# A two-layer hybrid trunk: 1024 output columns of layer one and the gates of layer two computed with tokens in rows, then turned and regrouped through DRAM

## The chip, the cores and the metric

The kernel runs on 1 core of one Trainium2 chip. The metric is device time in microseconds (us), the median of 3 runs. The profile is of one more execution of the same program, taken by the hardware profiler.

## What is computed

The input is x with 256 tokens of 2048 features, in f32. Two layers follow, each h = h + Mixer(RMSNorm(h)). The reference, cut to what matters here:

```python
# layer one (mixer A): gated DeltaNet with 16 heads of 128
proj = hn @ a_w_in                       # 2048 -> 8224: q, k, v (conv, SiLU), gate z, two scalars a head
o    = delta_rule(q, k, v, decay, beta)  # chunks of 64 tokens
h    = h + (rms_norm(o) * silu(z)) @ a_w_out          # 2048 -> 2048
# layer two (mixer B): chunked attention with 16 heads of 128
proj = rms_norm(h) @ b_w_in              # 2048 -> 8192: q, k, v, gate z
q, k = rms_norm(q), rms_norm(k)
p    = softmax(q @ k.T * scale + bias[relative distance], masked)
h    = h + ((p @ v) * silu(z)) @ b_w_out              # 2048 -> 2048
```

## The kernel before

**Chunks.** All four weight matrices are streamed once from DRAM in 320 chunks of 512 KB. A table, `plan`, lists them in order, and `chunk` consumes one after the other. A weight is split into two fp32r numbers: ScalarE casts it (`whi`, line 207), VectorE takes the difference (`wlo`, line 208), and TensorE adds three products, hi times hi, hi times lo and lo times hi (the matmuls of line 256). There are four buffers for `wt` and three each for `whi` and `wlo`. SyncE's DMA queue carries all weight loads. `fetch` runs three chunks ahead of the matmuls in the program.

**Three forms of a chunk.** Each covers 1024 weights of a partition and streams 6144 columns through TensorE:

- "features" (features in rows, tokens in columns): 24 matmuls of 256 columns, the weights stationary;
- "half" (features in rows): 8 matmuls of 512 columns, in which the high weights meet both parts of the activations at once, and 8 of 256. The two parts of the result are added afterwards by `joined` (ScalarE line 326, VectorE line 327);
- "tokens" (tokens in rows, features in columns): 12 matmuls of 512 columns, the activations stationary.

Counting from 0, the chunks of before are 0 to 7 features, 8 to 63 half, 64 to 87 tokens, 88 to 119 half, 120 to 127 tokens (all `a_w_in`), 128 to 143 features and 144 to 159 half (`a_w_out`), 160 to 191 half (gates of layer two), 192 to 255 tokens (keys and queries in four groups), 256 to 287 tokens (values) and 288 to 319 half (`b_w_out`).

**Two accumulators at once.** At the start of `a_w_out`, of layer two and of `b_w_out`, two PSUM blocks are first given three quarters of their sum each (`CUT` of `CPB` chunks, `CUTH` of `CPH`), so that the last quarter of the activations may come later. Then `drain` writes out all pending side work, and both blocks get their last quarter. PSUM has two such blocks (`psp`).

**Side work.** Norms, convolutions, attention and so on are generators in two lists, `bgq` and `bg2`. `step` takes a piece from one of the two in turn, between matmuls; `until(use)` holds a generator until the program has reached chunk `use`. The scheduler of the language then sets the order on each engine. Every engine executes in order, so an instruction that waits holds all behind it.

**After layer one.** `ha_small` adds a block of the `a_w_out` product to x (line 971, and 973 for the second part of a half), writes the split activations of layer two (`split`, lines 350 and 351) and sums squares (lines 361 to 364). `b_setup` makes the row scales. `zb_small` scales a gate block, loads a part of the attention bias (`relb`, GpSimd's DMA queue) and applies SiLU (line 1028).

**Round trips.** Keys, queries and attention weights are made with tokens in rows and needed with features in rows. `qk_norm` and `attend` turn blocks of 32 by 32 on VectorE (lines 1091 and 1150), write the result to DRAM with `trip` (line 1053, GpSimd's DMA queue) and load it regrouped with `back` (line 1059, four DMAs on SyncE's queue). `LEAD` is how many chunks after the end of a query block its scores begin. In `qk_norm` ScalarE copies the regrouped queries with a scale (line 1105).

**Values.** `vb_small` writes the values of a group of four heads to a part of `hmem["m"]` (line 1180), and `values` multiplies them with the attention weights (lines 1192 and 1194) and with the gate (line 1197).

Of the kernel before, what the change touches and what calls it, by code (L numbers as in the profile page):

```python
# [39 lines left out]
def tile_hybrid_trunk(  # L40
# [909 lines left out]
    def ha_small(n, ps, ks):  # L950

        if n == 0:
            m = slot("dl", 48)
            hmem["m"] = m
            hmem["h"] = m[:, :2 * D].rearrange("p (k t) -> p k t", k=KT)
            hmem["x"] = split_tiles()
            hmem["s"] = m[:, 8192:9216].rearrange("p (j t) -> p j t", j=4)
            hmem["done"] = 0
        xb, h, k0 = hmem["x"], hmem["h"][:, ks, :], ks.start
# [3 lines left out]
        two = len(ps.shape) == 4  # L963
        if two:
            ev = work.tile([P, 2, T], F32, name="ev", tag="ev")
            act.copy(out=ev, in_=ps[:, :, 1, :])
        yield 1
        if n < 2:

            dve.tensor_copy(out=hmem["h"][0:1, k0 + 8, 0:1], in_=ps[0:1, 0, 0:1])  # L970
        dve.tensor_tensor(out=h, in0=ps[:, :, 0, :] if two else ps, in1=h, op=ALU.add)
        if two:
            dve.tensor_tensor(out=h, in0=h, in1=ev, op=ALU.add)
# [73 lines left out]
    trips = [0]  # L1047

    def trip(u):

        trips[0] += 1
        m = rows.tile([P, 4, 32 * u.shape[1]], F32, name="trip%d" % trips[0])
        nc.gpsimd.dma_start(out=m, in_=u.rearrange("p x c j -> p c (x j)"))
        return m

    def back(dst, m):

        for c in range(4):
            nc.sync.dma_start(out=dst[32 * c:32 * c + 32].rearrange("i r x j -> i r (x j)"),
                              in_=m[:, c, :].rearrange("(r i) y -> i r y", r=4))  # L1060

    def until(use):

        while state["use"] < use:
            yield 0

# [249 lines left out]
```

## Time and profile before

| | |
|---|---|
| runs, us | 985.96, 985.99, 985.73 (median 985.96) |
| the profiled execution, us | 986.99, of which span 985.3 |
| TensorE busy | 978.8 us, 99% of the span |
| VectorE, ScalarE, GpSimd busy | 700.6 us (71%), 525.5 us (53%), 84.1 us (9%) |
| moved by DMA | 194.34 MB, mean 197 GB/s |

The profiled execution lies 1.03 us above the median of the runs. Matmuls are pipelined, so a "busy" TensorE may still be slowed by what feeds it; the pace of a stretch is read from how many matmuls start in it. P(i) below is the moment when the matmuls of chunk i end.

### The profile page before, as it was taken

How to read it: one execution, taken by the hardware profiler on the slowest of the kernel's cores; microseconds unless marked ns; L12 is line 12 of the kernel's file. 1: busy time of each engine (PE TensorE's matmuls, PEld its weight loads, DVE VectorE, ACT ScalarE, POOL GpSimd, SP SyncE). 2: the span in 40 equal slices, each digit the busy share in tenths (PEclk: the TensorE clock that was granted, in tenths of full speed). 3: DMA queues.
4: the chain of work that ended last, by engine and by line, in shares of the span. 5: the costliest groups of instructions: out<-in, count | busy, mean ns of one | idle time of the engine just before them, and what ended most of it. 6: DMA issues, size and time to landing. Idle time of an engine off the chain costs nothing.

```text
span 985.3 us, 15237 instructions
## 1 busy us (share of the span) xinstructions
PE 978.8 (99%) x5803; PEld 850.7 (86%) x5803; DVE 700.6 (71%) x1146; ACT 525.5 (53%) x741; POOL 84.1 (9%) x113
## 2 busy tenths in 40 slices
PE   9999999999999999999999999999999999999998
PEld 8988888888888889899988888888888788888887
DVE  7789787998989777665867555566858676655544
ACT  8455887645547645554655444445545445544442
POOL 1002100122000001010000000110212120000000
PEclk9999999999999999999999999999999999999999
DMA  9667775546665553446666777677979797765672
GB/s 294 193 170 234 217 202 164 170 131 189 173 193 154 158 159 110 128 129 225 224 193 179 221 222 211 174 248 222 282 220 291 211 299 209 214 192 171 211 223 80
DMA packets 149961, 194.34 MB, mean 197 GB/s; under 512 B 9328, under 2 KB 108032, under 8 KB 149888
## 3 DMA queue, kind: packets, MB, share of 16 engines
q1 hardware_dynamic: 146048, 179.47, 61.2%
q0 software_dynamic: 3552, 13.65, 4.0%
q8 instruction: 45, 0.74, 0.3%
q10 hardware_dynamic: 288, 0.26, 0.1%
q14 instruction: 28, 0.23, 0.1%
HBM read 183.90 MB, written 9.45 MB: 196 GB/s over the span
## 4 chain that ended last, share of the span: by engine, by line
PE 87%; DMA 5%; DVE 3%; ACT 2%; issue 1%; SPq 1%; POOL 0%; ACTq 0%; DVEq 0%
PE psp L256 78%; DMA wt<-in_b_w_in_dram 2%; PE pss L602 2%; DVE wlo L208 2%; DMA trip<-cv 1%; ACT whi L207 1%; DMA wt<-in_a_w_in_dram 1%; PE pss L256 1%; PE pss L839 1%; PE pss L1192 1%; DMA g<-in_xT_dram 1%; PE pss L1123 0%; PE pss L738 0%; PE pss L825 0%; PE pss L862 0%
## 5 line engine op out<-in xcount | busy, mean ns | idle before, releaser
L208 DVE TENSOR_TENSOR wlo<-wt,whi 128x1024 fp32r<-128x1024 f32 (+2 forms) x324 | 390.4, 1209 | 229.6 <-ACT whi L207 227.7
L207 ACT CAST whi<-wt 128x1024 fp32r<-128x1024 f32 (+2 forms) x324 | 336.0, 1039 | 348.0 <-PE psp L256 290.5
L256 PE MATMUL psp<-whi,xb 128*128 128x512 f32 x1024 | 325.2, 394 | 0.0
L256 PE MATMUL psp<-xb,whi 128*128 128x512 f32 (+1 forms) x1088 | 258.2, 380 | 0.2 <-DVE ev L327 0.2
L256 PEld LDWEIGHTS psp<-whi,xb 128*128 128x128 f32 x1024 | 191.9, 188 | 39.0
L256 PEld LDWEIGHTS psp<-xb,whi 128*128 128x128 f32 x1088 | 195.9, 190 | 34.2 <-DVE ev L327 0.6
L256 PE MATMUL psp<-wlo,xb 128*128 128x512 f32 x512 | 200.1, 391 | 0.5 <-DVE wlo L208 0.5
L256 PE MATMUL psp<-xb,wlo 128*128 128x256 f32 x1024 | 147.7, 285 | 0.6 <-DVE wlo L208 0.4
L256 PEld LDWEIGHTS psp<-xb,wlo 128*128 128x128 f32 x1024 | 137.0, 191 | 7.0 <-DVE wlo L208 1.8
L256 PE MATMUL psp<-g,whi 128*128 128x512 f32 (+1 forms) x608 | 131.6, 346 | 0.2 <-DVE ev L327 0.2
L256 PEld LDWEIGHTS psp<-g,whi 128*128 128x128 f32 x608 | 104.3, 190 | 13.0 <-DVE ev L327 0.6
L256 PEld LDWEIGHTS psp<-wlo,xb 128*128 128x128 f32 x512 | 96.2, 188 | 21.0 <-DVE wlo L208 1.6
L256 PE MATMUL psp<-g,wlo 128*128 128x256 f32 x480 | 82.2, 283 | 0.0
L256 PEld LDWEIGHTS psp<-g,wlo 128*128 128x128 f32 x480 | 69.8, 191 | 1.8
L519 DVE SCALAR_TENSOR_TENSOR cv<-raw,sm,cv 128x255 f32<-128x255 f32 (+2 forms) x144 | 63.9, 479 | 5.2 <-ACT cv L517 4.9
L517 ACT ACTIVATE cv<-raw,sm 128x256 f32<-128x256 f32 x48 | 22.1, 500 | 10.4 <-DVE raw L342 10.4
L327 DVE TENSOR_TENSOR ev<-psp,ev 128x512 f32<-128x512 f32 x37 | 25.2, 681 | 0.1
L1136 ACT ACTIVATE raw<-raw,mx 128x128 f32<-128x128 f32 (+1 forms) x32 | 14.3, 449 | 17.2 <-DVE mx L1134 17.1
L326 ACT COPY ev<-psp 128x512 f32<-128x512 f32 x37 | 21.4, 579 | 2.5 <-DVE raw L342 2.5
L874 POOL TENSOR_TENSOR ro<-so,nhalf 128x8 f32<-128x8 f32 x4 | 8.4, 2105 | 122.4 <-DVE so L872 122.4
L606 DVE TENSOR_TENSOR dl<-pss,dl 128x512 f32<-128x512 f32 (+1 forms) x32 | 16.4, 546 | 1.7 <-PE pss L602 1.7
L1077 POOL TENSOR_SCALAR ssn<-ssn,uh 128x4 f32<-128x4 f32 x16 | 8.2, 526 | 99.8 <-DVE ssn L1075 91.1
(243 smaller groups left out, 723.7 us busy)
## 6 DMA issues: line engine op xcount, KB each, us to landing
wt<-in_b_w_in_dram SPq DMA_DIRECT2D x128, 512.0 KB, 4.3
wt<-in_a_w_in_dram SPq DMA_DIRECT2D x125, 512.0 KB, 4.0
wt<-in_a_w_out_dram SPq DMA_DIRECT2D x32, 512.0 KB, 3.9
wt<-in_b_w_out_dram SPq DMA_DIRECT2D x32, 512.0 KB, 3.4
trip<-cv POOLq DMA_DIRECT2D x8, 512.0 KB, 5.3
trip<-dl POOLq DMA_DIRECT2D x8, 384.0 KB, 4.6
tt<-line POOLq DMA_DIRECT2D x4, 512.0 KB, 8.8
dl<-in_xT_dram POOLq DMA_DIRECT2D x4, 512.0 KB, 5.9
```

The source lines that it names most:

```text
L207: cast = act.copy(out=hi[:, js, cs], in_=wt[:, js, cs])
L208: rest = dve.tensor_tensor(out=lo[:, js, cs], in0=wt[:, js, cs], in1=hi[:, js, cs].bitcast(F32), op=ALU.subtract)
L256: state["mm"] = pe.matmul(*args, **kw).ins
L326: act.copy(out=ev, in_=ps[:, :, 1, :])
L327: dve.tensor_tensor(out=ev, in0=ps[:, :, 0, :], in1=ev, op=ALU.add)
L517: act.activation(out=cv[:, i, :], in_=raw[:, i, :], func=AF.Copy, scale=conv_w(i0 + i, 3))
L519: dve.scalar_tensor_tensor(out=cv[:, i, s:], in0=raw[:, i, :T - s], scalar=conv_w(i0 + i, 3 - s), in1=cv[:, i, s:], op0=ALU.mult, op1=ALU.add)
L602: pe.matmul(dst, lhsT=kq[:, a, i, c:c + P], rhs=rhs, start=(n == 0), stop=(n == 2))
L606: dve.tensor_tensor(out=dl[:, h, :, c], in0=src.rearrange("p (k c) -> p k c", k=2), in1=dec[:, h, c].unsqueeze(1).broadcast_to([P, 2, n]), ...
L839: pe.matmul(ps[:, i * P:(i + 1) * P], lhsT=tt[:, 2 * (h0 + i) + t, :], rhs=vb[:, i, t, :], start=True, stop=True)
L1136: act.activation(out=s[:, a:b], in_=s[:, a:b], func=AF.Exp, bias=mx[:, t:t + 1], accum_out=sums[:, t:t + 1])
L1192: pe.matmul(ps[:, 0:256].rearrange("p (x r j) -> p x r j", x=2, j=32), lhsT=v[:, 0, vs], rhs=pT0, start=True, stop=False)
```

## The change

The 1024 output columns of layer one that were in form features (16 chunks), and all 2048 gate columns of layer two that were in form half (32 chunks), are computed in form tokens. Their results have tokens in rows and are needed with features in rows. So VectorE turns them in blocks of 32 by 32 (`turn_tokens`), `trip` writes them to DRAM, and `back` loads them regrouped: six more round trips. For layer one, `ha_land` loads the regrouped block at `end + 4` and adds it to x at `end + 7`; `ha_split` is the rest of what `ha_small` did, and may now come in another order, for which `hmem["there"]` and `hmem["quads"]` keep count. For the gates, ScalarE applies SiLU with the row scale straight from PSUM, token rows being scaled by a number per partition, and `back` loads them at `end + 4`; the product in `values` reads the new layout. Further, `LEAD` goes from 11 to 12, the fetch of the attention weights comes one stage (two chunks) later, and the values of the four groups lie at 8192, 8192, 9216 and 10240 where they lay at 8192, 9216, 10240 and 11264.

```diff
-LEAD = 11
+LEAD = 12
...
-    plan += cut_halves(b_w_in, 6144)
+    for c0, c1 in ((0, CUT), (CUT, CPB)):
+        for j in range(2):
+            plan += wide(b_w_in, 6144 + 512 * j, c0, c1)
+    plan += wide(b_w_in, 7168) + wide(b_w_in, 7680)
...
+    def blocks(n):
+        return wk("cv").rearrange("p h t -> p (h t)")[:, :32 * 4 * n].rearrange("p (c x j) -> p x c j", c=4, j=32)
+    def turn_tokens(u, t, src):
+        dve.transpose(out=u[:, t::2], in_=src.rearrange("p (h c i) -> p h c i", c=4, i=32))
...
     def ha_small(n, ps, ks):
...
         if n < 2:
+            u = blocks(8)
+            for t in range(2):
+                turn_tokens(u, t, ps[:, t, :])
             dve.tensor_copy(out=hmem["h"][0:1, k0 + 8, 0:1], in_=ps[0:1, 0, 0:1])
-        dve.tensor_tensor(out=h, in0=ps[:, :, 0, :] if two else ps, in1=h, op=ALU.add)
...
+            yield 1
+            m = trip(u)
+            bg2.append(ha_land(ks, m, end))
+            return
...
+    def ha_land(ks, m, end):
+        yield from until(end + 4)
+        land = wk("cv").rearrange("p h t -> p (h t)").rearrange("p (r x j) -> p r x j", r=4, j=32)
+        back(land, m)
+        yield from until(end + 7)
+        h = hmem["h"][:, ks, :].rearrange("p k (t r j) -> p (k t) r j", t=2, r=4)
+        dve.tensor_tensor(out=h, in0=land.rearrange("p r x j -> p x r j"), in1=h, op=ALU.add)
+        yield 1
+        yield from ha_split(ks)
...
-    pa = [acc("features") for _ in range(2)]
+    pa = [acc("tokens") for _ in range(2)]
...
-                chunk("features", pa[j], gmem["b"], 2, ready(gmem))
+                chunk("tokens", pa[j], gmem["b"], 2, ready(gmem))
...
-    def zb_small(gi, evs):
-        z = bmem["z"][:, 4 * gi:4 * gi + 4, :]
-        scaled(z, evs, scales["h"][1])
+    def zb_small(gi, ps, end):
+        n, u = wk("cv").rearrange("p h t -> p (h t)").rearrange("p (t d) -> p t d", t=2), blocks(8)
+        for t in range(2):
+            act.activation(out=n[:, t, :], in_=ps[:, t, :], func=AF.Silu, scale=scales["h"][0][:, t:t + 1])
+        yield 1
...
-        act.activation(out=z, in_=z, func=AF.Silu)
+        for t in range(2):
+            turn_tokens(u, t, n[:, t, :])
+            yield 1
+        m = trip(u)
+        yield from until(end + 4)
+        back(bmem["z"][:, gi], m)
         yield 1
...
-    pb, evs = [acc("half") for _ in range(2)], []
-    for n in (CUTH, CPH - CUTH):
+    pb = [acc("tokens") for _ in range(2)]
+    for n in (CUT, CPB - CUT):
...
-                chunk("half", pb[j], xb, 2, ready(hmem))
-            if n != CUTH:
-                joined(pb[j], evs)
-    bgq.append(zb_small(0, evs))
-    for j in (1, 2, 3):
-        bgq.append(zb_small(j, pair(xb)))
+                chunk("tokens", pb[j], xb, 2, ready(hmem))
+            if n != CUT:
+                bgq.append(zb_small(j, pb[j], state["use"]))
+    for j in (2, 3):
+        bgq.append(zb_small(j, block("tokens", xb, 2), state["use"]))
...
-        stages = (scores, weights, turned, None, fetched_)
+        stages = (scores, weights, turned, None, None, fetched_)
...
-        c = 8192 + 1024 * gi
+        c = (8192, 8192, 9216, 10240)[gi]
...
+            z = bmem["z"][:, gi, :, h % 4 * 2:h % 4 * 2 + 2, :].rearrange("p r t j -> p t r j")
```

**SyncE's queue, from the start of `a_w_out`.** Before, nothing stands between the weight loads of `a_w_out` (`wt`) and the first keys of layer two:

```order
L181 DMA wt<-in_a_w_out_dram 128x2x512 x16
L181 DMA wt<-in_a_w_out_dram 128x4x256 x16
L181 DMA wt<-in_b_w_in_dram 128x4x256 x32
L181 DMA wt<-in_b_w_in_dram 128x2x512 x19
L1059 DMA dl<-trip_6421 32x4x256 x4
L181 DMA wt<-in_b_w_in_dram 128x2x512 x8
L1059 DMA cv<-trip_6588 32x4x256 x4
L181 DMA wt<-in_b_w_in_dram 128x2x512 x10
```

Of the change (`trip_4736` and `trip_4782` are the two blocks of layer one, the next two the first gates):

```order
L184 DMA wt<-in_a_w_out_dram 128x2x512 x16
L184 DMA wt<-in_a_w_out_dram 128x4x256 x6
L426 DMA cv<-trip_4736 32x4x256 x4
L184 DMA wt<-in_a_w_out_dram 128x4x256 x2
L426 DMA cv<-trip_4782 32x4x256 x2
L184 DMA wt<-in_a_w_out_dram 128x4x256
L426 DMA cv<-trip_4782 32x4x256 x2
L184 DMA wt<-in_a_w_out_dram 128x4x256 x7
L184 DMA wt<-in_b_w_in_dram 128x2x512 x23
L426 DMA tt<-trip_5535 32x4x256 x4
L184 DMA wt<-in_b_w_in_dram 128x2x512 x3
L426 DMA tt<-trip_5608 32x4x256 x4
```

The first loads of a round trip now stand behind the sixth half load of `a_w_out`, chunk 149, and the gates' first behind chunk 182 and chunk 185; all weight loads behind them wait with them.

**VectorE, after the first two blocks of layer one.** `wlo` rows are the weight differences, one a chunk, `xb` the split activations, `raw` the sums of squares. Before, the two blocks are added from PSUM at once, and the halves come after:

```order
L970 COPY dl<-psp 1x1
L971 TENSOR_TENSOR dl<-psp,dl 128x1024
L208 TENSOR_TENSOR wlo<-wt,whi 128x1024
L351 SCALAR_TENSOR_TENSOR xb<-dl,sm,xb 128x256 x4
L363 TENSOR_TENSOR raw<-raw 128x256 x2
L364 TENSOR_TENSOR dl<-raw 128x256
L208 TENSOR_TENSOR wlo<-wt,whi 128x1024
L970 COPY dl<-psp 1x1
L971 TENSOR_TENSOR dl<-psp,dl 128x1024
L208 TENSOR_TENSOR wlo<-wt,whi 128x1024 x2
L351 SCALAR_TENSOR_TENSOR xb<-dl,sm,xb 128x256 x4
L363 TENSOR_TENSOR raw<-raw 128x256 x2
```

Of the change, the blocks are turned at that place, and the sums come after the difference of chunk 150, together with those of the first halves:

```order
L440 STREAM_TRANSPOSE cv<-psp 128x4x4x32 x2
L998 COPY dl<-psp 1x1
L211 TENSOR_TENSOR wlo<-wt,whi 128x1024 x5
L1017 TENSOR_TENSOR dl<-cv,dl 128x1024
L1006 TENSOR_TENSOR dl<-psp,dl 128x512
L211 TENSOR_TENSOR wlo<-wt,whi 128x1024
L354 SCALAR_TENSOR_TENSOR xb<-dl,sm,xb 128x256
L1007 TENSOR_TENSOR dl<-dl,ev 128x512
L354 SCALAR_TENSOR_TENSOR xb<-dl,sm,xb 128x256 x3
L366 TENSOR_TENSOR raw<-raw 128x256 x2
L211 TENSOR_TENSOR wlo<-wt,whi 128x1024
L1017 TENSOR_TENSOR dl<-cv,dl 128x1024
```

and on from there:

```order
L354 SCALAR_TENSOR_TENSOR xb<-dl,sm,xb 128x256
L367 TENSOR_TENSOR dl<-raw 128x256
L354 SCALAR_TENSOR_TENSOR xb<-dl,sm,xb 128x256
L211 TENSOR_TENSOR wlo<-wt,whi 128x1024
L354 SCALAR_TENSOR_TENSOR xb<-dl,sm,xb 128x256
L211 TENSOR_TENSOR wlo<-wt,whi 128x1024
L354 SCALAR_TENSOR_TENSOR xb<-dl,sm,xb 128x256 x3
L1006 TENSOR_TENSOR dl<-psp,dl 128x512
L366 TENSOR_TENSOR raw<-raw 128x256 x2
L211 TENSOR_TENSOR wlo<-wt,whi 128x1024
```

The sums (L1017) and splits (L354) of the two blocks moved seven chunks down, to where the halves' own sums (L1006, L1007) and splits stand; from the first L1017 on there are 20 other instructions among five differences, chunks 151 to 155.

**ScalarE, where the queries of the third group arrive.** `dl<-cv,wqk` is the scaled copy of the regrouped queries; it waits for their load. Before:

```order
L207 CAST whi<-wt 128x1024 x7
L1072 ACTIVATE cv<-psp 128x1024
L1105 ACTIVATE dl<-cv,wqk 128x4x8x32
L207 CAST whi<-wt 128x1024 x3
L1136 ACTIVATE raw,sums<-raw,mx 128x128
```

Of the change:

```order
L210 CAST whi<-wt 128x1024 x7
L1110 ACTIVATE cv<-psp 128x1024
L1143 ACTIVATE dl<-cv,wqk 128x4x8x32
L210 CAST whi<-wt 128x1024 x3
L1174 ACTIVATE raw,sums<-raw,mx 128x128
```

The copy keeps its neighbours. Its place moved from behind the cast of chunk 250 to behind that of chunk 251, and on SyncE's queue the load of these queries moved likewise from behind the weights of chunk 251 to behind those of chunk 252.

More of the change, by code (lines that the diff above doesn't have):

```diff
@@ L409, in tile_hybrid_trunk, with trip, back, until @@
     rows = ctx.enter_context(tc.tile_pool(name="rows", bufs=1, space=bass.MemoryType.DRAM))
+    trips = [0]
+    def trip(u):
+        trips[0] += 1
+        m = rows.tile([P, 4, 32 * u.shape[1]], F32, name="trip%d" % trips[0])
+        nc.gpsimd.dma_start(out=m, in_=u.rearrange("p x c j -> p c (x j)"))
+        return m
+    def back(dst, m):
+        for c in range(4):
+            nc.sync.dma_start(out=dst[32 * c:32 * c + 32].rearrange("i r x j -> i r (x j)"),
+                              in_=m[:, c, :].rearrange("(r i) y -> i r y", r=4))
+    def until(use):
+        while state["use"] < use:
+            yield 0
+    def blocks(n):
+        return wk("cv").rearrange("p h t -> p (h t)")[:, :32 * 4 * n].rearrange("p (c x j) -> p x c j", c=4, j=32)
+    def turn_tokens(u, t, src):
+        dve.transpose(out=u[:, t::2], in_=src.rearrange("p (h c i) -> p h c i", c=4, i=32))
     dl = slot("dl", 48).rearrange("p (h k c) -> p h k c", h=H, k=2)
@@ L957, in ha_small @@
             hmem["s"] = m[:, 8192:9216].rearrange("p (j t) -> p j t", j=4)
-            hmem["done"] = 0
-        xb, h, k0 = hmem["x"], hmem["h"][:, ks, :], ks.start
+            hmem.update(done=0, quads=0, there=set())
+        h, k0, end = hmem["h"][:, ks, :], ks.start, state["use"]
         if k0 % 4 == 0:
@@ L962, in ha_small, with ha_split @@
             nc.gpsimd.dma_start(out=hmem["h"][:, qs, :], in_=xv[:, qs, :])
[L963 to L966, printed above, removed]
-        yield 1
[L968 to L973, printed above, removed]
-        yield 1
+        if n < 2:
+            u = blocks(8)
+            for t in range(2):
+                turn_tokens(u, t, ps[:, t, :])
+            dve.tensor_copy(out=hmem["h"][0:1, k0 + 8, 0:1], in_=ps[0:1, 0, 0:1])
+            yield 1
+            m = trip(u)
+            bg2.append(ha_land(ks, m, end))
+            return
+        ev = work.tile([P, 2, T], F32, name="ev", tag="ev")
+        act.copy(out=ev, in_=ps[:, :, 1, :])
+        yield 1
+        dve.tensor_tensor(out=h, in0=ps[:, :, 0, :], in1=h, op=ALU.add)
+        dve.tensor_tensor(out=h, in0=h, in1=ev, op=ALU.add)
+        yield 1
+        yield from ha_split(ks)
[7 more added lines that the diff above has]
+        yield 1
+        yield from ha_split(ks)
+    def ha_split(ks):
         for k in range(ks.start, ks.stop):
-            split(hmem["h"][:, k, :], k, 1, xb)
-            hmem["done"] = k + 1
+            split(hmem["h"][:, k, :], k, 1, hmem["x"])
+            hmem["there"].add(k)
+            while hmem["done"] in hmem["there"]:
+                hmem["done"] += 1
             yield 1
@@ L987, in b_setup @@
     def b_setup():
+        while hmem["quads"] < 4:
+            yield 0
         scales["h"] = yield from row_scales(hmem["s"], "rh")
@@ L1033, in tile_hybrid_trunk @@
     xb = hmem["x"]
-    pb, evs = [acc("half") for _ in range(2)], []
-    for n in (CUTH, CPH - CUTH):
+    pb = [acc("tokens") for _ in range(2)]
+    for n in (CUT, CPB - CUT):
         for j in range(2):
-            if n != CUTH and j == 0:
+            if n != CUT and j == 0:
                 drain()
             for _ in range(n):
-                chunk("half", pb[j], xb, 2, ready(hmem))
-            if n != CUTH:
-                joined(pb[j], evs)
-    bgq.append(zb_small(0, evs))
-    for j in (1, 2, 3):
-        bgq.append(zb_small(j, pair(xb)))
[L1047 to L1065, printed above, removed]
+                chunk("tokens", pb[j], xb, 2, ready(hmem))
[3 more added lines that the diff above has]
+        bgq.append(zb_small(j, block("tokens", xb, 2), state["use"]))
     def qk_norm(ps, scale, dst, end):
```

8 lines of the change are left out of this document (5 added, 3 removed).

## The prediction

> **What bounds the kernel now.** First the page, then the table of who waited for whom.
>
> ```profile
> span 985.3 us, 15237 instructions
> PE 978.8 (99%) x5803; PEld 850.7 (86%) x5803; DVE 700.6 (71%) x1146; ACT 525.5 (53%) x741; POOL 84.1 (9%) x113
> ...
> ACT whi L207 <- PE psp L256: 290.5, 185, 5.2
> DVE wlo L208 <- ACT whi L207: 227.7, 171, 6.3
> ...
> ACT dl L1105 <- DMA cv<-trip: 12.3, 3, 4.5
> ```
>
> TensorE is busy for 99% of the span. ScalarE's casts wait 290.5 us for TensorE to free a weight buffer, and VectorE's differences wait for the casts: the side engines wait for TensorE. So the pace of its matmuls sets the time, and a stall elsewhere counts only where it outlasts the lead of the weights. The pace of the three forms is read from three stretches without other matmuls (windows: length, busy time with the number of instructions, clock, DMA):
>
> ```profile
> 452.10:472.26 20.16, 20.16 (x171) 20.16 (x170) 11.63 (x16) 10.16 (x15) 0.75 (x1) 1.00 0.74 247
> 562.76:607.30 44.54, 44.54 (x258) 39.37 (x256) 24.56 (x26) 20.64 (x22) 1.70 (x5) 1.00 0.71 213
> 610.02:664.42 54.40, 54.40 (x242) 45.06 (x240) 32.43 (x32) 23.90 (x23) 7.97 (x9) 1.00 0.71 213
> ```
>
> The columns are TensorE, its weight loads, VectorE, ScalarE and GpSimd. Two or three matmuls in each were under way at its left edge; 168, 256 and 240 start in it, which are 7, 16 and 20 chunks. So a chunk takes 20.16 / 7 = 2.88 us in form features, 44.54 / 16 = 2.784 in form half and 54.40 / 20 = 2.72 in form tokens. All stream 6144 columns; a matmul of 512 columns starts every 54.40 / 240 = 0.2267 us, one of 256 every 20.16 / 168 = 0.120, and not every 0.113. In the features stretch weight loads are busy all the time (20.16 of 20.16), in the tokens stretch 83%.
>
> **The matmuls.** 16 chunks go from features to tokens: 16 x (2.88 - 2.72) = 2.56 us less. 32 go from half to tokens: 32 x (2.784 - 2.72) = 2.03 us less. All lie on the bound; together -4.59.
>
> Here a rule speaks against the change. The Trainium skill ("TensorE: Matmul & The Clock Gate", section Back-to-back issue gap) gives N / 2.4 + 2.5 ns for the isolated gap of N columns: 215.8 ns for 512 and 109.2 for 256, nearly proportional to the columns. By it the estimate of the saving is 16 x 31 + 32 x 10 ns = 0.83 us. The trace has 226.7 and 120 ns, and I take the trace.
>
> **The gap at the gates' drain.** Two eights of 512-column matmuls follow on eights of 256; the last one doesn't:
>
> ```profile
> 535.36 2.00 PE L256 MATMUL psp<-xb,whi 128*128 128x512 f32 x8
> 537.20 1.11 PE L256 MATMUL psp<-xb,wlo 128*128 128x256 f32 x8
> 538.16 2.00 PE L256 MATMUL psp<-xb,whi 128*128 128x512 f32 x8
> 540.37 2.11 PE L256 MATMUL psp<-xb,whi 128*128 128x512 f32 x8 [0.21 <-DVE ev L327]
> ...
> 539.63 0.68 DVE L327 TENSOR_TENSOR ev<-psp,ev 128x512 f32<-128x512 f32 x1
> ```
>
> An eight takes 537.20 - 535.36 = 1.84 us, here 540.37 - 538.16 = 2.21: 0.37 us in which chunk 168 waits for the PSUM block that `joined` has just read. With tokens that block is complete after chunk 173 and is needed for chunk 176, two chunks or 5.4 us later. -0.37 (bounds 0 and -0.5).
>
> **Work added beside.** The nearest rows (groups by line, mean ns of one behind the comma):
>
> ```profile
> L1091 DVE STREAM_TRANSPOSE cv<-cv 128x512 f32<-128x512 f32 x16 | 10.8, 686 | 0.0
> L773 ACT ACTIVATE kT<-psp,rx 128x512 f32<-128x512 f32 x8 | 5.0, 680 | 3.5 <-PE pss L602 3.5
> L971 DVE TENSOR_TENSOR dl<-psp,dl 128x1024 f32<-128x1024 f32 x2 | 2.4, 1202 | 0.0
> L971 DVE TENSOR_TENSOR dl<-psp,dl 128x512 f32<-128x512 f32 x4 | 2.7, 682 | 0.0
> L973 DVE TENSOR_TENSOR dl<-dl,ev 128x512 f32<-128x512 f32 x4 | 2.8, 688 | 0.1
> L351 DVE SCALAR_TENSOR_TENSOR xb<-dl,sm,xb 128x256 fp32r<-128x256 f32 x16 | 6.8, 475 | 1.2 <-ACT xb L350 1.2
> L363 DVE TENSOR_TENSOR raw<-raw 128x256 f32<-128x256 f32 x16 | 6.0, 417 | 0.2 <-ACT raw L361 0.2
> L208 DVE TENSOR_TENSOR wlo<-wt,whi 128x1024 fp32r<-128x1024 f32 x317 | 386.3, 1222 | 227.7 <-ACT whi L207 225.8 <-PE psp L256 0.7 <-issue 0.2
> ...
> 717.42 1.23 DVE L208 TENSOR_TENSOR wlo<-wt,whi 128x1024 fp32r<-128x1024 f32 x1 [1.50 <-ACT whi L207]
> 716.34 1.05 ACT L207 CAST whi<-wt 128x1024 fp32r<-128x1024 f32 x1 [1.67 <-PE psp L256]
> ```
>
> In the gates, VectorE gets 8 transposes of 0.69 us (if one out of PSUM costs like one out of SBUF, between 0.69 and, as the dearest VectorE row here, 1.22) and loses 8 joins and 8 scalings of that size; ScalarE gets 8 SiLUs of 0.68 for 8 copies and 4 larger SiLUs. VectorE is busy 24.56 of 44.54 us there: nothing on the path. Without that cover 8 x 0.69 = 5.5 us would come in.
>
> How much cover is there? A cast starts as chunk i - 3 ends and the difference ends 2.31 us later (716.34 to 718.65), while chunk i begins after two more chunks, 5.44 us: a lead of about 3.1 us.
>
> After layer one that is tight. From the first regrouped sum, VectorE has 20 instructions among five differences: 2 x 1.20 + 2 x 0.68 + 0.69 + 10 x 0.475 + 5 x 0.42 + 5 x 1.22 = 17.4 us, against five half chunks of 13.9. The backlog of 3.5 us shrinks by nearly 0.1 per instruction that starts while another ends, and grows by ScalarE waits inside the string. Against 3.1 of lead that costs 0 to 1.5 us. Before, the two blocks and the halves came seven chunks apart, so the densest five chunks were lighter. I take +0.4, nearer the lower end, since means overstate a full queue.
>
> **Six round trips and the queues they pass.**
>
> ```profile
> wt<-in_b_w_in_dram SPq DMA_DIRECT2D x128, 512.0 KB, 4.3
> trip<-cv POOLq DMA_DIRECT2D x8, 512.0 KB, 5.3
> cv<-trip SPq DMA_DIRECT2D x16, 128.0 KB, 5.7
> ...
> 717.20 1.73 SPq L1059 DMA_DIRECT2D cv<-trip  x4
> ```
>
> On SyncE's queue the first regrouped load stands behind weights 149, which go out when difference 145 ends: P(142) + 2.3 = P(141) + 5.0. Its trip starts at about P(141) + 1.6 (two transposes and a start) and lands 5.3 later, at +6.9. So the queue waits 1.9 us, all weights behind it too, then issues four loads in 1.73. Weights 150, due at P(143) + 2.3 = P(141) + 7.7, go out 0.9 late. A weight load has 4 x 2.72 - 2.31 - 4.3 = 4.3 us to spare, so this costs nothing; if the spare were gone, each us late would cost one. The gates' trips come out alike: the first goes out about 4.0 after P(173) (a cast of 1.05, two SiLUs, two transposes), and its loads stand behind weights 182, at P(175) + 2.3 = P(173) + 7.7. The first block of layer one is regrouped at about P(141) + 6.9 + 1.7 + 5.7 = P(141) + 14.3 and first used after difference 150, at P(147) + 2.3 = P(141) + 18.9; were it later than that, the sum would hold differences 151 and on behind it. GpSimd's queue gets six issues (the bias loads and x loads stand there too); nothing on the path waits for it. New values buffers: the second group waits for the first group's matmuls, which end three chunks earlier in the order: 0.
>
> **LEAD and the later stage.** What happens now where regrouped queries arrive (SyncE, then ScalarE, VectorE, TensorE):
>
> ```profile
> 713.95 2.06 SPq L1059 DMA_DIRECT2D kT<-trip  x4
> ...
> 724.88 1.16 ACT L1105 ACTIVATE dl<-cv,wqk 128x1024 f32<-128x1024 f32 x1 [3.85 <-DMA cv<-trip]
> ...
> 728.28 0.50 PE L256 MATMUL psp<-wlo,xb 128*128 128x512 f32 x1 [0.20 <-DVE wlo L208]
> ...
> 779.83 0.22 PE pss L1122 x2
> 780.05 0.43 PE pss L1123 x2
> ...
> 721.58:737.03 15.45, 15.24 (x69) 12.39 (x68) 9.08 (x17) 7.03 (x10) 3.22 (x3) 1.00 0.65 205
> ...
> 768.33:784.44 16.11, 15.52 (x69) 12.31 (x68) 9.07 (x17) 6.96 (x10) 3.22 (x3) 1.00 0.74 216
> ```
>
> SyncE waits until 713.95 for the weights' trip, the queries' loads come behind it, ScalarE waits 3.85 us, and TensorE waits for the next difference. The two windows hold five chunks and two heads of scores (0.22 + 0.43 us each in the chain), 13.6 + 2 x 0.65 = 14.9 us: 0.55 and 1.2 lost. For the third group I set 0.9 between them, 2.65 in all. In the changed order the queries' copy is one chunk later, but so are the weights' trip before it and the loads on SyncE's queue. The wait goes along: 0. Bounds: -2.65 if the chunk is won against the load, +1.5 if the third wait, now in front of four heads of values, grows.
>
> **Sum.** -2.56 - 2.03 - 0.37 + 0.4 + 0 = -4.56. On the profiled execution (986.99 with 1.7 around its span of 985.3) that gives 982.4 and a span of 980.7; on the median of 985.96, which lies 1.03 lower, 981.4 us.
>
> **Rivals.**
> - *The waits for queries go* as well: 981.4 - 2.65 = 978.75. For it: the copy is a chunk (2.72 us) later and the waits are 12.3 in three. Against: all three places moved together. 0.15.
> - *VectorE or the loads pile up* between layers: 2 to 3 us instead of 0.4, 983 to 984. For it: DMA is 74% busy there at 247 GB/s before a trip comes in. Against: the margins of 4.3 and 3.1 us. 0.15, a third of it within 0.2%.
> - *The forms cost alike*, TensorE being paced by columns: 985.96 - 0.37 + 0.4 = 986.0. Against: the three windows. The skill's gap, cited above, is near this. 0.03.
> - *Slower*: each of the six new trips makes the weights late as a queries' trip does now. At 1.2 us each, 7.2 - 4.96 = +2.2: 988.2. It is slower by more than 0.2% from 1.15 us a trip on. For it: the same pattern on the same queue costs that much at 768. Against: here SyncE waits about 2 us of 4.3 to spare, and in the gates nothing on ScalarE or VectorE waits for the landing. 0.06.
>
> **Numbers.** The sum itself has 0.57, with a range of its own of 980.3 to 983.0; 0.04 is left for what I don't see, counted as no change. A change under 0.2% (2 us) is about what a measurement can't tell from none. Faster: 0.57 + 0.15 + 0.10 = 0.82; same 0.05 + 0.03 + 0.04 = 0.12; slower 0.06. From 978.6 to 984.5 the range holds the first three cases.
>
> **What would show it.** In the changed profile the `a_w_out` blocks and the gates should start a matmul every 0.2267 us, 48 chunks of 2.72; the gap at the gates' drain is gone; differences 151 to 157 end late, with up to half a us lost there; SyncE's waits for trips grow by about six times 2 us without late weights; the queries' waits stay near 12 us. I am wrong if tokens out of layer one's gated values run slower than 2.72, or if weights come late in the gates.

## The result: 980.28 us, and the profile after

The changed kernel takes 980.28 us (runs from 979.39 to 982.84) against 985.96: the ratio is 0.9948, with a 95% interval from 0.9933 to 0.9962. That is 5.7 us less; 4.6 were forecast, to 981.4. Run again beside other kernels it took 980.40, against 985.27 for the kernel before in that session: 4.9 us less. In four later sessions the kernel before took 985.17 to 985.30, so about 0.7 of the 5.7 us look like the first session's and not the change's. The profiled execution took 979.39, the fastest of its runs, while that of before lies above its median, so the two profiles differ by more (span 985.3 to 977.7) than the medians do.

The page of the changed kernel:

```profile
span 977.7 us, 14649 instructions
PE 971.6 (99%) x5483; PEld 833.8 (85%) x5483; DVE 698.8 (71%) x1142; ACT 521.8 (53%) x737; POOL 86.0 (9%) x119
```

The waits on ScalarE and on SyncE's queue (total, times, longest). L210, L211, L426 and L1143 are lines 207, 208, 1059 and 1105 of before:

```profile
ACT whi L210 <- PE psp L259: 319.4, 202, 5.2
...
ACT dl L1143 <- DMA cv<-trip: 4.4, 3, 2.0
```

```profile
SPq L426 <- DMA trip<-cv: 25.7, 14, 4.1
...
SPq L426 <- DMA trip<-dl: 13.5, 8, 2.5
```

ScalarE waits longer for TensorE (319.4 against 290.5 us) and less for the queries (4.4 against 12.3). To place the 7.6 us, here are four windows: chunks 128 to 143, 144 to 159, 160 to 191 and 224 to 287, each from the first matmul of its first chunk to that of the next. The columns are length, TensorE, weight loads, VectorE, ScalarE, GpSimd, clock, DMA share, GB/s. Before:

```profile
420.00:472.26 52.26, 52.26 (x442) 52.26 (x441) 32.40 (x48) 26.01 (x35) 5.82 (x5) 1.00 0.59 189
472.26:516.82 44.56, 44.56 (x259) 39.35 (x257) 31.25 (x41) 24.75 (x37) 0.75 (x1) 1.00 0.65 204
516.82:607.30 90.48, 90.27 (x522) 79.52 (x520) 53.84 (x62) 42.49 (x49) 4.22 (x11) 1.00 0.68 204
696.40:889.37 192.97, 192.17 (x869) 159.01 (x868) 127.94 (x235) 94.09 (x142) 23.38 (x28) 1.00 0.80 239
```

After:

```profile
419.08:468.88 49.80, 49.80 (x249) 42.23 (x248) 30.62 (x42) 23.15 (x27) 6.39 (x6) 1.00 0.62 195
468.88:513.42 44.54, 44.54 (x257) 39.36 (x256) 34.58 (x50) 27.37 (x45) 1.29 (x2) 1.00 0.89 255
513.42:601.45 88.03, 88.03 (x393) 73.00 (x392) 49.03 (x53) 39.76 (x45) 6.74 (x13) 1.00 0.79 245
690.55:881.72 191.17, 191.17 (x870) 159.31 (x868) 129.51 (x238) 94.72 (x146) 20.59 (x28) 1.00 0.79 242
```

The 16 chunks of `a_w_out` gave 2.46 us, the gates 2.45, the stretch of attention 1.80; chunks 144 to 159, where the turned blocks land, cost nothing although their DMA share rose from 0.65 to 0.89. Chunk 128 begins 0.92 us earlier, in code that is the same: in the thirteen profiles of this study it began anywhere from 419.1 to 420.3 us, whatever the kernel. The four sum to 6.73, with that 7.65: the whole difference of the spans.

So two terms of the forecast came as costed, and two differ: the LEAD part shows 1.80 us where 0 was set, and the string of work after layer one cost 0 where 0.4 was set. The experiments ask about these two. They are named by what they do; "part" is a part of the change done alone.

### The profile page after: what moved, and what is told of

Same layout as the page of the kernel before. It is cut to its first block, busy times and chain, and to the rows that moved or that the text cites. A ratio compares the mean times of both kernels' runs of the same rounds, so it can differ in the third digit from the quotient of the medians.

```text
span 977.7 us, 14649 instructions
## 1 busy us (share of the span) xinstructions
PE 971.6 (99%) x5483; PEld 833.8 (85%) x5483; DVE 698.8 (71%) x1142; ACT 521.8 (53%) x737; POOL 86.0 (9%) x119
## 4 chain that ended last, share of the span: by engine, by line
PE 97%; ACT 1%; DMA 1%; issue 0%; DVE 0%; SPq 0%
PE psp L259 87%; PE pss L633 2%; PE pss L259 1%; PE pss L870 1%; PE pss L1161 1%; PE pss L1230 1%; DMA g<-in_xT_dram 1%; ACT whi L210 0%; PE pss L769 0%; PE pss L856 0%; PE pss L891 0%; PE pss L892 0%; PE pss L893 0%; PE pss L877 0%; PE pss L1232 0%
## 5 line engine op out<-in xcount | busy, mean ns | idle before, releaser
L211 DVE TENSOR_TENSOR wlo<-wt,whi 128x1024 fp32r<-128x1024 f32 (+2 forms) x324 | 392.1, 1213 | 224.3 <-ACT whi L210 221.1
L210 ACT CAST whi<-wt 128x1024 fp32r<-128x1024 f32 (+2 forms) x324 | 336.3, 1040 | 374.7 <-PE psp L259 319.4
L259 PE MATMUL psp<-whi,xb 128*128 128x512 f32 x1280 | 403.9, 393 | 0.0
L259 PEld LDWEIGHTS psp<-whi,xb 128*128 128x128 f32 x1280 | 239.9, 188 | 49.0
L259 PE MATMUL psp<-wlo,xb 128*128 128x512 f32 x640 | 250.0, 391 | 0.0
L259 PE MATMUL psp<-xb,whi 128*128 128x512 f32 (+1 forms) x832 | 195.4, 376 | 0.5 <-ACT whi L210 0.5
L259 PEld LDWEIGHTS psp<-xb,whi 128*128 128x128 f32 x832 | 148.4, 189 | 25.0 <-ACT whi L210 0.7
L259 PE MATMUL psp<-xb,wlo 128*128 128x256 f32 x768 | 113.4, 285 | 0.6 <-DVE wlo L211 0.5
L259 PE MATMUL psp<-g,whi 128*128 128x512 f32 x352 | 85.3, 392 | 0.2 <-DVE ev L330 0.2
L259 PEld LDWEIGHTS psp<-g,whi 128*128 128x128 f32 x352 | 64.5, 188 | 12.9 <-DVE ev L330 0.6
L259 PE MATMUL psp<-g,wlo 128*128 128x256 f32 x352 | 46.0, 283 | 0.0
L259 PE MATMUL psp<-whi,g 128*128 128x512 f32 x128 | 40.2, 392 | 0.0
```

What stands on the lines that cost most here:

```text
L210: cast = act.copy(out=hi[:, js, cs], in_=wt[:, js, cs])
L211: rest = dve.tensor_tensor(out=lo[:, js, cs], in0=wt[:, js, cs], in1=hi[:, js, cs].bitcast(F32), op=ALU.subtract)
L259: state["mm"] = pe.matmul(*args, **kw).ins
```

## Experiments on LEAD and the queries' waits

**The third part alone**, on the kernel before:

```diff
-LEAD = 11
+LEAD = 12
...
-        stages = (scores, weights, turned, None, fetched_)
+        stages = (scores, weights, turned, None, None, fetched_)
...
-        c = 8192 + 1024 * gi
+        c = (8192, 8192, 9216, 10240)[gi]
```

> The kernel before with the third part of the change alone: LEAD 12, the fetch of the attention weights one stage later, the values in the other buffers; all forms as before. Theory A (this part won, because the queries' loads get one chunk of room and land earlier): chunks 224 to 287 take 1.80 us less, as they did in the changed kernel (191.17 us against 192.97), no difference of theirs ends after the chunk before it, and the time is about 984.2 us. Theory B (the wait goes along, as predicted; the 1.80 us come from the new forms, which move the work in front): the waits of ScalarE for the regrouped queries stay near 12 us, chunks 224 to 287 stay at 193.0 +- 0.3 us, the time within 0.3 us of 986.

**The forms alone**: the changed kernel with these three edits undone.

```diff
-LEAD = 12
+LEAD = 11
...
-        stages = (scores, weights, turned, None, None, fetched_)
+        stages = (scores, weights, turned, None, fetched_)
...
-        c = (8192, 8192, 9216, 10240)[gi]
+        c = 8192 + 1024 * gi
```

> The changed kernel with LEAD 11, the stages and the values' buffers of before; a_w_out and gates in tokens remain. Theory A: chunks 128 to 143 take 49.8 us and 160 to 191 take 88.0, as in the changed kernel, chunks 224 to 287 go back to 193.0, so about 1.8 us slower than the changed kernel, near 982. Theory B: everything as in the changed kernel, chunks 224 to 287 at 191.2 us and about 980.3.

**The gates alone**: that, and `a_w_out` in features with the old `ha_small`.

```diff
-    pa = [acc("tokens") for _ in range(2)]
+    pa = [acc("features") for _ in range(2)]
...
-                chunk("tokens", pa[j], gmem["b"], 2, ready(gmem))
+                chunk("features", pa[j], gmem["b"], 2, ready(gmem))
```

> The kernel before with only the 32 gate chunks in tokens (a_w_out in features, LEAD 11, stages and values of before). Both theories: chunks 160 to 191 take 88.0 us against 90.5, so 2.4 us less and a time near 983.5; were the gain of the gates owed to the a_w_out blocks ahead of them (an earlier x for layer two), it would be less than 1 us here. Chunks 224 to 287 stay at 193.0 by theory A.

Measured on the same chip, with 985.27 for before: the third part 984.97 (ratio 0.9997, 0.9988 to 1.0006), the forms 980.53 (0.9950, 0.9938 to 0.9962), the gates 982.53 (0.9973, 0.9963 to 0.9983). The stretch of chunks 224 to 287 in the third part alone, then in the forms alone, then in the gates alone (below its stretch of gates):

```profile
695.87:887.04 191.17, 191.17 (x870) 159.23 (x868) 129.21 (x238) 94.75 (x146) 20.47 (x28) 1.00 0.78 242
```

```profile
691.22:882.45 191.23, 191.23 (x869) 159.26 (x868) 128.67 (x235) 94.64 (x142) 23.04 (x28) 1.00 0.78 241
```

```profile
516.48:604.51 88.03, 88.03 (x394) 72.96 (x392) 49.02 (x53) 39.80 (x45) 6.69 (x13) 1.00 0.78 245
693.61:884.84 191.23, 191.23 (x870) 159.21 (x869) 128.03 (x235) 94.38 (x142) 23.01 (x28) 1.00 0.79 241
```

All three have the short stretch, two of them with LEAD 11. Neither theory foresaw that: theory A said that the forms alone would go back to 193.0, and theory B that the third part alone would not move. The gates alone confirm their own price: 88.03 us, and 2.7 us in the medians. But the third part alone gained 1.8 us in the profile and nothing measurable in the medians. So I asked whether the first profile of before was typical.

**The kernel before, once more.**

> The kernel before once more, for a second profile. In its first profile, TensorE lost 1.80 us in chunks 224 to 287, where ScalarE waited 3.85, 4.51 and 3.94 us for the regrouped queries. The kernel with only the gates in tokens, which keeps LEAD 11, waited 2.26, 3.23 and 3.80 us and lost nothing there. Theory A (chance: the waits of the old order lie between 2 and 4.5 us from one execution to the next, and TensorE loses only what goes beyond about 3.8): the waits differ from 3.85, 4.51 and 3.94 by up to 2 us, and chunks 224 to 287 take between 191.2 and 193. Theory B (gates in form half lengthen these waits): chunks 224 to 287 take 193.0 +- 0.2 us again.

It took 986.05 us, and its stretch 192.06, between the two values. ScalarE's waits for the queries in that profile (start and length, shape, wait):

```profile
723.59 1.15 ACT L1105 ACTIVATE dl<-cv,wqk 128x1024 f32<-128x1024 f32 x1 [2.62 <-DMA cv<-trip]
770.05 1.15 ACT L1105 ACTIVATE dl<-cv,wqk 128x1024 f32<-128x1024 f32 x1 [2.79 <-DMA cv<-trip]
817.83 1.15 ACT L1105 ACTIVATE dl<-cv,wqk 128x1024 f32<-128x1024 f32 x1 [4.63 <-DMA cv<-trip]
```

The first two were 3.85 and 4.51 in the first profile and cost TensorE 0.5 and 1.1 us there; at 2.62 and 2.79 they cost nothing, and only the third did (0.84). Theory A holds as far as chance goes: how long a wait is, and whether it costs TensorE anything, differs from one execution to the next. Its edge of about 3.8 us is only rough, since 3.85 us in the first place cost 0.5 and 3.94 in the third 0.2. Of the 1.80 us, 0.9 was the luck of one profile.

**LEAD 10**, on the changed kernel, with the stages of before:

```diff
-LEAD = 12
+LEAD = 10
...
-        stages = (scores, weights, turned, None, None, fetched_)
+        stages = (scores, weights, turned, None, fetched_)
```

> The changed kernel with LEAD 10 and the stages of before, two chunks less room than it has. Theory A (the lead of the queries' copy is a cushion: each chunk less lengthens ScalarE's wait by 1 to 1.5 us, and TensorE loses what goes beyond 3.8): waits of 3.5 to 6 us in the three places, chunks 224 to 287 take 193 to 196 us against 191.2, the time 2 to 4 us longer than the changed kernel's. Theory B (the wait goes along, whatever LEAD is): the waits stay at 2 to 3 us, chunks 224 to 287 at 191.2, the time near 980.5.

It took 980.60 us (0.9952, 0.9940 to 0.9965), no different from the changed kernel. The waits in its profile, and those of the changed kernel:

```profile
716.34 1.15 ACT L1143 ACTIVATE dl<-cv,wqk 128x1024 f32<-128x1024 f32 x1 [4.18 <-DMA cv<-trip]
761.58 1.15 ACT L1143 ACTIVATE dl<-cv,wqk 128x1024 f32<-128x1024 f32 x1 [3.15 <-DMA cv<-trip]
809.34 1.15 ACT L1143 ACTIVATE dl<-cv,wqk 128x1024 f32<-128x1024 f32 x1 [4.63 <-DMA cv<-trip]
```

```profile
717.84 1.16 ACT L1143 ACTIVATE dl<-cv,wqk 128x1024 f32<-128x1024 f32 x1 [0.86 <-DMA cv<-trip]
765.72 1.15 ACT L1143 ACTIVATE dl<-cv,wqk 128x1024 f32<-128x1024 f32 x1 [1.53 <-DMA cv<-trip]
812.12 1.15 ACT L1143 ACTIVATE dl<-cv,wqk 128x1024 f32<-128x1024 f32 x1 [2.00 <-DMA cv<-trip]
```

The waits are as theory A said, the time is not: 2 to 4 us were expected, and in this profile chunks 192 to 287 took 280.69 us against 280.27 (the first heads of scores now come before chunk 224). The mean wait is 3.99 us with LEAD 10 (one profile), 3.19 with 11 (four) and 2.00 with 12 (eight): a chunk of 2.72 us more LEAD takes about 1 us off a wait. Most of it does go along, since `qk_norm` hangs the loads (`end + LEAD - 4`) and the copy (`end + LEAD - 1`) on the same number. The edge moves along too, that is, how long a wait may be before TensorE loses anything (its cover). In these profiles the longest wait that cost nothing was 4.18 us with LEAD 10, 3.80 with 11 and 2.71 with 12; the shortest that cost 0.1 us or more was 4.63, 3.85 and 2.89. So a chunk more of LEAD shortens the wait and its cover alike, and the time hardly shows it. Why the cover shrinks was not tested. Near the edge chance decides: with LEAD 11 a profile lost between 0 and 1.8 us there, with 12 between 0 and 2.1.

## Experiments on the stretch where the blocks land

**The changed kernel, once more.**

> The changed kernel once more, for a second profile and its times on the same chip as the parts. The profiled spans differ by 7.6 us, the medians by 5.7. Theory A (the rest is the weather of the first chunks): chunks 128 to 317 take the same as in the first profile within 0.2 us, and what differs between executions lies before chunk 64, where the changed kernel is the same as before. Theory B (the changed stretches themselves vary, since the six trips collide with weights in some executions): chunks 128 to 191 are longer than 49.8, 44.5 and 88.0 us by 1 us or more in this profile, or in that of the forms alone.

Neither theory is whole. Most of it repeats (49.80, 88.02 and 191.42 us in the three other stretches), but chunks 144 to 159 took 46.09 us, 1.55 more than in the first profile, and 44.88 with the forms alone. The place in this profile: SyncE's load of weights 150 (the first of the two), ScalarE's cast of them, TensorE at the start of chunk 153, and the DMA engines while it happens (window):

```profile
472.64 1.84 SPq L184 DMA_DIRECT2D wt<-in_a_w_out_dram  x2
482.71 1.05 ACT L210 CAST whi<-wt 128x1024 fp32r<-128x1024 f32 x1 [5.22 <-DMA wt<-in_a_w_out_dram]
```

```profile
495.33 1.21 PE L259 MATMUL psp<-g,wlo 128*128 128x256 f32 x8 [1.28 <-DVE wlo L211]
```

```profile
468.86:480.00 11.14, 11.14 (x66) 9.85 (x65) 6.15 (x7) 4.22 (x4) 1.30 (x2) 1.00 1.02 322
```

The order of events: two trips, their regrouped loads and two loads of x meet the weights from 469 to 480, the DMA engines are busy all the time, and weights 150, issued at 472.6, land at 482.6. Over all loads of `b_w_in` the median from issue to landing is 4.3 us (page of before). Here are the loads of `a_w_out` issued from 468 to 484, before and in the first profile of the change (count, size, median us to landing):

```profile
wt<-in_a_w_out_dram SPq DMA_DIRECT2D x6, 512.0 KB, 4.8
```

```profile
wt<-in_a_w_out_dram SPq DMA_DIRECT2D x6, 512.0 KB, 9.4
```

The cast is 2.5 us behind its turn, VectorE's string of sums, splits and squares comes behind it, and the difference of chunk 153 is 1.28 us late for TensorE. In the first profile the same cast waited too, but 1.5 us less:

```profile
481.18 1.05 ACT L210 CAST whi<-wt 128x1024 fp32r<-128x1024 f32 x1 [3.67 <-DMA wt<-in_a_w_out_dram]
```

and the same difference ended 0.16 us before its use: nothing was lost, by a hair.

**One x load later.** `ha_small` delays the loads of x with a one-element copy; the last is now held for the third block instead of the second:

```diff
         if n < 2:
...
-            dve.tensor_copy(out=hmem["h"][0:1, k0 + 8, 0:1], in_=ps[0:1, 0, 0:1])
+            if n == 0:
+                dve.tensor_copy(out=hmem["h"][0:1, k0 + 8, 0:1], in_=ps[0:1, 0, 0:1])
...
+        if n == 2:
+            dve.tensor_copy(out=hmem["h"][0:1, 12, 0:1], in_=ps[0:1, 0, 0, 0:1])
```

> The changed kernel with the load of the last quarter of x hooked to the third a_w_out block instead of the second, so that 512 KB leave the stretch in which both trips, their regrouped loads and two x loads meet the weights (DMA share over 1, weights 150 land after 9 to 10 us). Theory A (weights 150 and 151 come late because the DMA engines are full there, and VectorE's string of splits then ends late): cast 150 waits at least 1 us less, the difference of chunk 153 ends 0.7 us or more ahead of its use, chunks 144 to 159 take 44.5 us where the two profiles of the changed kernel had 44.5 and 46.1, and the time is 0.3 to 1 us lower. Theory B (the regrouped loads on SyncE's queue ahead of weights 150 are what makes them late): cast 150 is as late as before, time near 980.4.

```profile
481.42 1.05 ACT L210 CAST whi<-wt 128x1024 fp32r<-128x1024 f32 x1 [2.70 <-PE psp L259]
```

Cast 150 waits for TensorE again and not for its weights; the difference of chunk 153 ends 1.12 us ahead of its use, the stretch takes 44.55 us, and the kernel 980.11 (0.9949, 0.9936 to 0.9962). Theory B is refuted, since the regrouped loads still stand ahead of weights 150; theory A holds in the cast and the stretch. But the DMA engines are no emptier here:

```profile
470.09:481.23 11.14, 11.14 (x66) 9.84 (x65) 6.09 (x6) 4.21 (x4) 0.56 (x1) 1.00 1.02 325
```

```profile
wt<-in_a_w_out_dram SPq DMA_DIRECT2D x6, 512.0 KB, 7.8
```

The share is 1.02 as in the second profile. What 512 KB less of x changed is the landing: weights 150 needed 7.5 us where they had needed 9 to 10. The gain of 0.3 us in the median is less than these runs can tell.

**All of a_w_out in tokens.** The other four half blocks of `a_w_out` become two tokens blocks, with the same `ha_land`:

```diff
-    plan += halves(a_w_out, 1024, 4)
+    plan += wide(a_w_out, 1024) + wide(a_w_out, 1536)
...
-    for j in range(4):
-        a_done(j + 2, block("half", gmem["b"], 2), 8 + 2 * j, 10 + 2 * j)
+    for j in (2, 3):
+        a_done(j, block("tokens", gmem["b"], 2), 4 * j, 4 * j + 4)
```

> The changed kernel with the other 16 a_w_out chunks in tokens too (all 2048 columns turned and regrouped, eight new trips instead of six). By the pace, 16 x (2.784 - 2.72) = 1.0 us less in chunks 144 to 159, 43.5 us. Theory A (room enough: the last block lands at chunk 166 and its last quarter is first used at chunk 172): time near 979.4, since no block of four additions and its joins stands in VectorE's string any more. Theory B (the new trips pile up with the first gate chunks): chunks 160 to 175 longer than 44.0 by 1 us or more, and no gain.

No gain: 981.62 us (0.9962, 0.9949 to 0.9976), with runs from 979.36 to 983.69. The profiled one took 979.95; three others took 2.9 to 3.7 us more, and what cost them that is open, since none has a profile. The trouble is earlier than theory B put it, in the stretch itself, which is denser now:

```profile
468.98:514.03 45.05, 44.11 (x194) 35.88 (x192) 30.27 (x39) 23.35 (x35) 1.85 (x3) 1.00 0.94 267
```

```profile
482.13 1.05 ACT L210 CAST whi<-wt 128x1024 fp32r<-128x1024 f32 x1 [3.74 <-DMA wt<-in_a_w_out_dram]
```

**The same, with two x loads later**, each held for its own block:

```diff
+        if n > 1:
+            dve.tensor_copy(out=hmem["h"][0:1, k0, 0:1], in_=ps[0:1, 0, 0:1])
         if k0 % 4 == 0:
...
-        if n < 2:
-            dve.tensor_copy(out=hmem["h"][0:1, k0 + 8, 0:1], in_=ps[0:1, 0, 0:1])
```

> All 2048 columns of a_w_out in tokens, as in the run before, and the last two x loads hooked to the third and fourth a_w_out block, so that 1 MB leaves the stretch of the first two trips. In the run before, weights 150 to 154 were cast 2.3 to 4.1 us after the chunk that frees their buffer, and chunks 144 to 159 took 45.05 us where 43.5 were expected. Theory A (full DMA engines made those weights late): casts 150 and 151 start within 0.5 us of the chunk that frees them, chunks 144 to 159 take 43.5 to 43.8 us, and the time is 979.3 with runs within 1 us of each other, where the run before had 979.4 to 983.7. Theory B (the string of splits on VectorE is too dense for five tokens chunks of 2.72 us whatever the weights do): differences 152 to 154 still end late, chunks 144 to 159 take 44.5 or more, near 980.4.

```profile
469.09:512.61 43.52, 43.52 (x193) 36.04 (x192) 29.78 (x38) 22.93 (x34) 1.84 (x3) 1.00 0.86 263
469.09:480.23 11.14, 11.14 (x51) 9.23 (x50) 6.09 (x6) 4.28 (x5) 0.54 (x1) 1.00 0.92 287
```

```profile
480.17 1.05 ACT L210 CAST whi<-wt 128x1024 fp32r<-128x1024 f32 x1 [1.67 <-PE psp L259]
```

The 16 chunks take 16 x 2.72 = 43.52 us, without any loss, and the kernel 979.13 (0.9939, 0.9925 to 0.9952; runs from 978.45 to 979.85, a little wider than expected): theory A, in the stretch, in the cast and in the time. VectorE's string is hardly shorter (29.78 us busy against 30.27); it fits when the weights are on time.

**Half of b_w_out in tokens too.** `b_w_out`'s first 16 chunks in tokens, then turned, regrouped, added to h and stored:

```diff
-    plan += cut_halves(b_w_out, 0)
+    for c0, c1 in ((0, CUT), (CUT, CPB)):
+        for j in range(2):
+            plan += wide(b_w_out, 512 * j, c0, c1)
+    plan += halves(b_w_out, 1024, 4)
...
+            if n != CUT:
+                bg2.append(out_tokens(j, po[j], state["use"]))
```

> The same, and the first 16 of the 32 b_w_out chunks in tokens too, turned and regrouped, added to h and stored. By the pace, 16 x 0.064 = 1.0 us less in chunks 288 to 303, and the gap of 0.5 us at the drain of b_w_out (chunk 296) may go as the gates' one did, so 1.0 to 1.5 us less than the run without it, near 978. Theory B (the two trips come where the attention of the last heads and the output stores stand on SyncE's queue): weights come late there and the gain is less than 0.5 us.

983.12 us (0.9979, 0.9970 to 0.9988): 4 us slower than without it. The first 16 chunks gave what was expected, the next eight (second row) took it back and more, by an order on VectorE that neither theory had thought of:

```profile
881.14:927.32 46.18, 46.18 (x209) 38.45 (x208) 23.65 (x26) 19.50 (x22) 0.54 (x1) 1.00 0.59 190
927.32:956.33 29.01, 25.30 (x130) 21.91 (x128) 14.56 (x14) 8.89 (x9) 0.54 (x1) 0.88 0.79 249
```

```profile
937.12 1.22 DVE L1281 TENSOR_TENSOR cv<-cv,dl 128x1024 f32<-128x1024 f32 x1
940.87 1.30 DVE L443 STREAM_TRANSPOSE cv<-psp 128x512 f32<-128x512 f32 x2
```

```profile
942.33 3.75 PE L262 MATMUL psp<-g,whi 128*128 128x512 f32 x8 [3.71 <-DVE cv L443]
```

Both blocks were put in one list of side work, in which a generator that waits for a chunk holds the next. So the second block was turned only after the first had landed and been added (L1281), and TensorE waited for its PSUM block.

**Turning and landing in two lists**, as layer one has them:

```diff
-        m = trip(u)
-        yield from until(end + 4)
+        bg2.append(out_land(n, trip(u), end))
+
+    def out_land(n, m, end):
+        yield from until(end + 4)
...
-                bg2.append(out_tokens(j, po[j], state["use"]))
+                bgq.append(out_tokens(j, po[j], state["use"]))
```

> The same with the turning of the two b_w_out blocks in the first list of side work and only the regrouped load and the sum in the second, as layer one has it. In the run before, the second block was turned only after the first had been regrouped and added (940.87 against 922.08), TensorE waited 3.71 us for that PSUM block, and chunks 304 to 311 took 29.0 us. Theory A (that order alone took back the gain): chunks 304 to 311 take 22.3 us, 288 to 303 stay at 46.2, and the time is 979.1 - 1.5 = 977.6. Theory B (the trips make weights late at the end as well): chunks 304 to 311 stay 1 us or more above 22.3.

```profile
690.54:883.77 193.23, 191.80 (x870) 159.15 (x868) 128.98 (x238) 94.56 (x146) 20.62 (x28) 1.00 0.78 239
883.77:929.96 46.19, 46.19 (x210) 38.45 (x209) 23.66 (x26) 19.50 (x22) 0.54 (x1) 1.00 0.59 190
929.96:952.22 22.26, 22.26 (x129) 19.68 (x128) 14.37 (x14) 8.91 (x9) 0.54 (x1) 1.00 0.96 301
```

977.10 us, ratio 0.9915 (0.9901 to 0.9929): theory A, and the fastest version here, below both kernels (8.2 us below the kernel before in its session). Its profiled execution, 979.53, was the slowest of five (the other four: 976.89 to 977.14), and the first row says where: 193.23 us in the attention, the queries' wait once more, with LEAD 12:

```profile
767.88 1.16 ACT L1138 ACTIVATE dl<-cv,wqk 128x1024 f32<-128x1024 f32 x1 [3.71 <-DMA cv<-trip]
815.27 1.15 ACT L1138 ACTIVATE dl<-cv,wqk 128x1024 f32<-128x1024 f32 x1 [4.10 <-DMA cv<-trip]
```

## Why the prediction was right, point by point

- **The matmuls: right.** -2.56 was forecast for `a_w_out`, -2.46 measured; -2.03 and the gap of -0.37 for the gates, -2.45 measured. 32 x 2.72 = 87.04 us leaves 0.99 in the 88.03 of the gates, the matmuls of layer two's row scales in chunks 165 and 167; no gap is left. The parts alone say the same in the medians: 2.7 us for the gates, and 2.0 more with `a_w_out`, where the landing takes some back. The rival that the forms cost alike (986.0) is refuted: 48 chunks gave 4.9 us in both profiles, of which 0.4 is the gap at the drain. The estimate of 0.83 us of saving by the Trainium skill ("TensorE: Matmul & The Clock Gate", section Back-to-back issue gap) came out far too low; the section itself says that its formula for the isolated gap leaves out the weight loads and counts too little at few columns, which the prediction passed over. At 512 columns the section says that it counts too much, and there the trace differs: 226.7 ns against 215.8. Why a matmul of 256 columns starts only every 0.120 us was not tested: that weight loads were busy all the time there is a likely reason and not a shown one.
- **VectorE's string after layer one: right in place and size, half wrong in cause.** +0.4, between 0 and 1.5, was forecast for differences 151 to 157. The four profiles with both forms as changed and the x loads in place lost 0 (the first one, and LEAD 10), 0.3 and 1.5 us (the second one), in the main in front of chunk 153; "up to half a us" was too little for the last. The step that failed is the one on weights: that a weight load has 4.3 us to spare, "so this costs nothing", took the landing of 4.3 us from the median over all loads of `b_w_in`. That they go out 0.9 us late was right; but in the crowded stretch weights 150 needed 9 to 10 us, used up all the spare time, and then the string began late. So it is the loads of the rival "VectorE or the loads pile up" that did it, at 0 to 1.5 us where the rival set 2 to 3.
- **LEAD and the later stage: 0 was within what the runs can tell (-0.3 us, interval -1.2 to +0.6), but the argument was not.** That "the queries' waits stay near 12 us" is wrong: they were 4.4 and 6.3 in sum, against 12.3 and 10.0. That "all three places moved together" was no reason; about a third of each chunk of LEAD is won. The term still came out near 0, as the cover of a wait shrank along with it, which the prediction did not see: that is luck. The loss of 2.65 us that I read from one profile was 1.80 (the third wait cost 0.2, not the 0.9 that I had set between the others) and mostly a draw of that execution. The rival "the waits for queries go", at 978.75, is what the first profile of the change shows, and not what the medians show.
- **Round trips and the queues: right in the waits and the time, wrong on late weights.** SyncE's waits for trips out of `cv` grew from 15.5 to 25.7 us; six times 2 was forecast. But "without late weights" did not hold, after layer one (above) or in the gates, where the first gate's regrouped loads stand ahead of weights 183. Their cast in the first profile of the change, then in the second:

```profile
572.61 1.05 ACT L210 CAST whi<-wt 128x1024 fp32r<-128x1024 f32 x1 [2.55 <-DMA wt<-in_b_w_in_dram]
```

```profile
574.79 1.05 ACT L210 CAST whi<-wt 128x1024 fp32r<-128x1024 f32 x1 [3.20 <-DMA wt<-in_b_w_in_dram]
```

These weights needed 8.5 and 8.9 us to land, and the cast came 0.9 and 1.5 us behind its turn. The prediction had named that as a sign of being wrong. Its price did not follow, since the lead of about 3.1 us covers it: the stretch took 88.03 and 88.02 us, with nothing lost, so the slower rival, 1.2 us for each trip, did not happen in the four trips of the gates.

## What to carry to other kernels

Price a moved form by how many matmuls start in a clean stretch, and take the landing time of a load from the stretch where it will stand, not from a median over the whole kernel: a 512 KB load needed about 4 us as a rule and 9 to 10 where round trips and loads of x met it. The share of busy DMA engines does not tell the two apart well: at the same 1.02 a load of that place took 10.0 us in one run and 7.5 in another. Before a stall is put in a sum, look at a second profile: a wait that ends near the edge of its cover costs 2 us in one execution and nothing in the next. And a step that turns a PSUM block must not stand behind one that waits for a landing.

## What the runs showed of the hardware

I had not expected what a pause of TensorE costs. In the run where it waited 3.71 us for the transpose, the granted clock fell in the pause and stayed low behind it (windows of that run, the clock is the third number from the end):

```profile
936.62:938.60 1.98, 1.98 (x10) 1.32 (x8) 1.72 (x2) 0.00 (x0) 0.00 (x0) 1.00 0.86 275
...
942.33:945.20 2.87, 2.87 (x7) 2.29 (x8) 1.11 (x2) 0.00 (x0) 0.54 (x1) 0.50 1.00 366
945.20:948.00 2.80, 2.80 (x13) 2.61 (x12) 0.12 (x1) 1.04 (x1) 0.00 (x0) 0.50 0.38 125
...
950.00:952.00 2.00, 2.00 (x10) 1.62 (x10) 0.92 (x1) 1.04 (x1) 0.00 (x0) 1.00 0.78 261
```

From 941.59, 3 us into the pause, to 948.42, 6.1 us after TensorE had resumed, it was half, so the eight matmuls of 512 columns there took 3.75 us instead of 2.00, and the stretch lost 29.01 - 22.26 = 6.75 us, almost twice the pause. The Trainium skill ("TensorE: Matmul & The Clock Gate", section What's actually happening) says that the clock is halved after at least one idle window of about 3.4 us and comes back after at least one busy window of that length. This case agrees in the main: the pause of 3.71 us halved it, though the fall came already 3 us into it, and the pauses of 1.3 us and less in the other profiles left the clock at 1.00. The edge itself was not measured. A stall on TensorE is worth its own length only while it is short.
